# Experts' outputs of a mixture of experts: from a table in DRAM to sums on the chip, with all lists of 32 places

## The chip, the core and the metric

The kernel runs on one core of a Trainium2 chip. The metric is device time in microseconds (us) of one execution. The core has five engines that run side by side and wait for each other by semaphores: TensorE (PE; its weight loads are shown as PEld), VectorE (DVE), ScalarE (ACT), GpSimd (POOL) and SyncE (SP, which here only starts transfers). Products go to PSUM, eight banks of 512 numbers in each of 128 partitions; SBUF holds the rest.

## The reference

Two blocks one after the other on 512 tokens of 1024 numbers; only the end of the second is touched:

```
def hierarchical_moe(h, ...):                 # h: rmsnorm of x, 512 tokens
    grp = argmax(group_logits)                # one of 4 groups
    top_val, top_idx = top_k(expert_logits of that group, 2)
    gate = p_grp * softmax(top_val)
    # every token goes to 2 of 32 experts
    a = xb @ w_gate[e]; u = xb @ w_up[e]      # 1024 -> 512, twice
    y = (silu(a) * u) @ w_down[e]             # 512 -> 1024
    out[token] += y * gate
x = x + hierarchical_moe(rmsnorm(x), ...)
return rmsnorm(x, final_norm_g)
```

The inputs are drawn once, and so the routing is fixed. Counted from the reference on these inputs, 28 of 32 experts get tokens. Ten get more than 32: 179, 118, 109, 94, 70, 68, 66, 64, 48 and 38; the other 18 get 1 to 29.

## The kernel before

The mixture of experts comes last. Its three stages follow each other: routing (`route_block`, `order`), a loop over experts (`expert`), and `combine`.

**Routing** makes, by products with 0/1 matrices, a list of tokens for every expert: the first 32 places in one table, the places beyond in a second one, in blocks of 64. The experts are put in an order by their counts (`place`), so that large and small ones alternate; the largest is the seventh (e = 6), the last four have no tokens and are skipped.

**The loop.** The weights of an expert are three pieces of 2 MB: gate and up (two pieces, `wgu`) and down (`wdn`). They stand in a ring of 10 pieces (`self.ring`); `reload` has SP start piece q + 10 once piece q was used, with at most four 1 MB transfers under way. For each expert:

- `gather` (POOL starts it, four experts ahead) fetches the rows of the 32 tokens from `h2d`; each token is four rows of 256 numbers, so that 4 x 32 partitions are filled. `to_t` transposes them (PE) and scales them (DVE).
- `gate_up` makes the products with gate and up: 32 matmuls of 32 tokens by 256 columns, four side by side in the 128 columns of the array (the trace shows two instructions for each fp32 product). ACT takes the silu, DVE multiplies (`a`), `act_t` transposes (PE) and copies (DVE).
- `down` makes the products with down (16 matmuls), ACT copies them to `yo`, and POOL writes the rows to a table in DRAM, `yd`, at an address for each (token, choice) (`yi`).
- `down` of expert e runs one step late, after `gate_up` of e + 1 (`prev`), while ACT and DVE work on e + 1.
- `more` handles the places beyond 32 in blocks of 64, under `tc.If(n > b)`. An expert with few tokens jumps over this code. A block is 32 matmuls for gate and up in two halves, two transposes, 8 matmuls of 512 columns for down, and a write to `yd`.

**`combine`** reads all of `yd` (4 MB), multiplies by the gates, adds both choices to the residual `self.x` (DVE, ACT and POOL), takes the rms norm and writes the result.

The order of instructions on each engine in the loop is the order of the code (`tc.manual_schedule`).

Of the kernel before, what the change touches and what calls it, by code (L numbers as in the profile page):

```python
# [76 lines left out]
class Kern:  # L77
# [951 lines left out]
    def moe_open(self):  # L1029
# [10 lines left out]
        self.yd = self.dp.tile([8 * T, 256], F32, name="yd")  # L1040
# [7 lines left out]
        self.spacer = mp.tile([1, 1], F32, name="spacer")  # L1048
# [3 lines left out]
        self.part = mp.tile([128, 2], I32, name="part")  # L1052
        self.off = mp.tile([128, 2], F32, name="off")
        for i, n in enumerate((4, 2)):
            for g in range(n):
                r = slice(g * 128 // n, (g + 1) * 128 // n)
                nc.vector.memset(self.part[r, i:i + 1], g)
                nc.vector.memset(self.off[r, i:i + 1], float(2048 * n + g))

        self.yi, self.xi = [[mp.tile([128, 32], I32, name=f"{nm}0")] for nm in ("yi", "xi")]  # L1060
        self.hv = (self.h2d, self.h2d.rearrange("(r h) c -> r (h c)", h=2))
# [9 lines left out]
    def route_consts(self, cp):  # L1071
# [7 lines left out]
        self.iota = cp.tile([128, 2, 128], F32, name="iota")  # L1079
        for i, n in enumerate((4, 2)):  # L1080
            nc.gpsimd.iota(self.iota[:, i], pattern=[[0, n], [1, 128 // n]], base=0, channel_multiplier=0,
                           allow_small_or_imprecise_dtypes=True)
# [13 lines left out]
        self.val = cp.tile([128, NB, 2], F32, name="val")  # L1096
        nc.gpsimd.iota(self.val, pattern=[[256, NB], [1, 2]], base=-2048, channel_multiplier=2,
# [40 lines left out]
    def route_block(self, tb):  # L1138


        nc, mp, sm = self.nc, self.ro, self.sm
# [14 lines left out]
        le = mp.tile([128, 3, 32], F32, name="le", tag="le", bufs=2)  # L1156
# [10 lines left out]
        V.tensor_scalar(m[:, 4:8], self.iota[:, 0, 0:4], m[:, 0:1], NEG, op0=ALU.not_equal, op1=ALU.mult)  # L1167
        yield 1
        V.tensor_tensor(le[:, 0].rearrange("p (g e) -> p g e", g=4), lg[:, 8:40].rearrange("p (g e) -> p g e", g=4),
                        m[:, 4:8, None].to_broadcast([128, 4, 8]), op=ALU.add)  # L1170
        yield 1
        V.max(r[:, 8:16], le[:, 0])
        yield 1
        V.max_index(ix[:, 8:16], r[:, 8:16], le[:, 0])
# [3 lines left out]
        for k in range(2):  # L1178
            V.tensor_scalar(le[:, 1 + k], self.iota[:, 0, 0:32], m[:, 1 + k:2 + k], None, op0=ALU.is_equal)
        yield 1  # L1180
        V.tensor_tensor(self.OH[:, tb], le[:, 1], le[:, 2], op=ALU.add)
# [5 lines left out]
        for k in range(2):  # L1187
            V.scalar_tensor_tensor(le[:, 0], p[:, 0:32], 1.0, le[:, 1 + k], op0=ALU.mult, op1=ALU.mult,
                                   accum_out=m[:, 8 + k:9 + k])
# [3 lines left out]
        for k in range(2):  # L1193
            row = mp.tile([128, 128], F32R, name="row", tag=f"row{k}", bufs=2)
            V.tensor_scalar(row, self.iota[:, 0], m[:, 8 + k:9 + k], None, op0=ALU.is_equal)
            col = mp.tile([128, 32], F32R, name="col", tag=f"col{k}", bufs=2)
            V.tensor_scalar(col, le[:, 1 + k], self.val[:, tb, k:k + 1], None, op0=ALU.mult)
            ends = dict(stop=tb == NB - 1 and k == 1, skip_group_check=True)
            mm(self.pt[0][:, 0:4], row, col[:, 0:4], start=tb == 0 and k == 0, **ends)
            mm(self.pt[0][0:32, 128:256], col, row, start=False, **ends)  # L1200
        yield 1
        if tb == NB - 1:
            self.index(0, self.pt[0][:, 0:3], slice(0, 3))
            self.gather(self.xg0, self.xi[0][:, 0:1], 4)
# [3 lines left out]
        V.tensor_scalar(n[:, 18:20], n[:, 16:18], 63, None, op0=ALU.bitwise_and)  # L1208
        V.tensor_scalar(n[:, 20:22], n[:, 16:18], 6, None, op0=ALU.logical_shift_right)
# [3 lines left out]
        for k in range(2):  # L1213
            E = (V, P)[k]
            row = mp.tile([128, 128], F32R, name="rowb", tag=f"row{k}", bufs=2)
            V.tensor_scalar(row, self.iota[:, 1], m[:, 10 + k:11 + k], None, op0=ALU.is_equal)
            bv = mp.tile([128, 8], F32, name="bv", tag=f"bv{k}", bufs=2)
            E.tensor_scalar(bv, self.iota[:, 0, 0:8], m[:, 12 + k:13 + k], self.val[:, tb, k:k + 1], op0=ALU.is_equal,
                            op1=ALU.mult)
            col = mp.tile([128, 8, 32], F32R, name="colb", tag=f"colb{k}", bufs=2-k)  # L1220
            E.tensor_tensor(col, le[:, 1 + k, None, :].to_broadcast([128, 8, 32]),
                            bv[:, :, None].to_broadcast([128, 8, 32]), op=ALU.mult)
            for i in range(2):
                mm(self.pt[1][:, i * 128:i * 128 + 128], col[:, i * 4:i * 4 + 4, :].rearrange("p b e -> p (b e)"), row,
                   start=tb == 0 and k == 0 and i == 0, stop=tb == NB - 1 and k == 1, skip_group_check=True)

    def xindex(self, x, y, i, n):
        V = self.nc.vector
        V.tensor_scalar(x, y, 3 - i, 2 - i, op0=ALU.logical_shift_right, op1=ALU.logical_shift_left)
        V.tensor_tensor(x, x, self.part[:, i:i + 1].to_broadcast([128, n]), op=ALU.bitwise_or)  # L1230

    def index(self, i, src, c):

        y, x = self.yi[i], self.xi[i]
        self.nc.vector.tensor_scalar(y[:, c], src, (4.0, 2.0)[i], self.off[:, i:i + 1], op0=ALU.mult, op1=ALU.add)
        c = slice(c.start, min(c.stop, x.shape[1]))
        self.xindex(x[:, c], y[:, c], i, c.stop - c.start)

    def gather(self, xg, ix, G):
        self.nc.gpsimd.indirect_dma_start(out=xg, out_offset=None, in_=self.hv[G == 2],  # L1240
                                          in_offset=bass.IndirectOffsetOnAxis(ap=ix, axis=0),
                                          bounds_check=G * T - 1, oob_is_err=False)

    def gates(self, mp):
# [10 lines left out]
        V.tensor_tensor(self.gate[:, :, 1:2], self.gate[:, :, 0:1], g[:, :, 4:5], op=ALU.mult)  # L1255

# [15 lines left out]
    def moe(self):  # L1272
        nc, tc, A = self.nc, self.tc, self.A
        mm, V = nc.tensor.matmul, nc.vector
        self.shut()
        with self.pool("moe3") as m3:
            self.ring.append(m3.tile([128, 4, 1024], F32, name="ring9"))
            R, LV, LAST = 10, 3, 28
            self.yi.append(m3.tile([128, 256], I32, name="yi1"))
            self.xi.append(m3.tile([128, 32 * LV], I32, name="xi1"))  # L1280
            yi, xi, index, xindex, gather, hv = self.yi, self.xi, self.index, self.xindex, self.gather, self.hv

            def order(place, eno):
# [4 lines left out]
                T0, T1, k = xhs[2][0:32, 0:128], xhs[2][:, 128:384], xhs[2][:, 384:448]  # L1288
                nc.scalar.copy(T0, self.pt[0][0:32, 128:256])
                nc.scalar.copy(T1, self.pt[1][:, 0:256])  # L1290
# [9 lines left out]
                perm, cn = xtv[:, 0:128], xtv[0:32, 128:256]  # L1300
                V.tensor_scalar(perm, place.rearrange("p b e -> p (b e)"), own[:, 3:4], None, op0=ALU.is_equal)
                V.tensor_copy(cn, own[0:32, 0:1].to_broadcast([32, 128]))
                p = self.ps("at", "tables")
                mm(p[:, 0:32], T0, perm[0:32, 0:32], start=True, stop=True, skip_group_check=True)
                for i in range(2):
                    mm(p[:, 32 + i * 128:160 + i * 128], T1[:, i * 128:i * 128 + 128], perm, start=False, stop=True,
                       skip_group_check=True)
                for i, l in enumerate((cn, eno)):
                    mm(p[:, 288 + i * 32:320 + i * 32], l, perm[0:32, 0:32], start=False, stop=True,
                       skip_group_check=True)  # L1310
                index(0, p[:, 3:32], slice(3, 32))
                index(1, p[:, 32:288], slice(0, 256))
                return p[:, 288:352]
            yv = (self.yd, self.yd.rearrange("(r h) c -> r (h c)", h=2))
            xgs = [self.xg0] + [m3.tile([128, 256], F32, name=f"xga{i}") for i in range(1, 4)]
            xhs = [m3.tile([128, 512], F32, name=f"xgb{i}") for i in range(3)]
            xtn = m3.tile([128, 4, 2, 64], F32, name="xtn")
            xtv = xtn.rearrange("p i g t -> p (i g t)")
            ysts = []


            def to_t(xg, G, xt=None):

                n = KT // G
                xt = xt or m3.tile([128, n, G, 128 // G], F32, name="xt", tag=f"xt{G}", bufs=2)
                p = self.ps("at", "tp")
                for i in range(n):
                    nc.tensor.transpose(p[:, i * 128:i * 128 + 128], xg[:, i * 128:i * 128 + 128], self.ident)
                gv = self.gT.rearrange("p (g i) -> p i g", i=n)
                V.tensor_tensor(xt, p[:, 0:n * 128].rearrange("p (i g t) -> p i g t", i=n, g=G),  # L1330
                                gv[:, :, :, None].to_broadcast([128, n, G, 128 // G]), op=ALU.mult)
                return xt

            def gate_up(e, xt, G, p, q):

                n, W, C = KT // G, 128 // G, 1024 // G
                c = q * 256
                for kt in range(KT):
                    w = self.ring[(3 * e + kt // 4) % R]
                    for g in range(G):  # L1340
# [452 lines left out]
```

## Time and profile before

| what | value |
|---|---|
| median of 3 runs | 2059.64 us (2058.2 to 2063.69) |
| profiled execution, own time | 2060.64 us |
| its span, first to last instruction | 2058.9 us |
| PE busy | 1873.5 us (91%) |
| routing and lists made, about | 1541 to 1580 us |
| loop over experts | 1580.5 to 2024.5 us |
| after the last product | 2024.5 to 2058.9 us |

The span is what the rows below are counted in; 1.7 us of the profiled execution lie around it. A busy PE is one that has a matmul under way, which can be one that waits for weights or goes at half clock.

### The profile page before, as it was taken

Reading aid. Unit: us, or ns where it says so; the run is one execution under the profiler, and the core shown is the slowest. Engines: PE = TensorE matmul, PEld = TensorE weight load, DVE = VectorE, ACT = ScalarE, POOL = GpSimd, SP = SyncE. Lnnn points to the kernel's source line nnn. Section 1 sums busy time; section 2 is a strip of 40 time slices with the busy share of each in tenths; the row PEclk is TensorE's granted clock in tenths of the full one; section 3 lists DMA queues with packets and bytes.
Section 4 is the critical chain, followed back from the end, with each engine's and each line's share of the span. In section 5 each row is a group of like instructions: output and inputs, shape, how many; then the busy total and the mean of one; then the engine's idle time right before and its main releaser. Section 6 shows DMA issues by size and latency. Waiting matters only on the chain. (4 is left out here: it accounts for less than half of the span.)

```text
span 2058.9 us, 28841 instructions
## 1 busy us (share of the span) xinstructions
PE 1873.5 (91%) x11078; PEld 1432.5 (70%) x11082; DVE 950.0 (46%) x1700; ACT 764.0 (37%) x1197; POOL 335.7 (16%) x344
## 2 busy tenths in 40 slices
PE   8999999999999999899999998899896698878882
PEld 6777878888887888778888887677674354444441
DVE  5556375444436457565454436676655011101113
ACT  6547334333322577724333323455641000000002
POOL 0001111111002100011111001455112112222212
PEclk9999999999999999999999999899797799999996
DMA  5221233322232522133232232222075999999994
GB/s 184 86 82 48 86 111 97 101 98 97 92 103 77 167 66 99 36 113 99 96 96 98 92 103 72 77 82 82 32 290 200 399 374 391 390 374 415 410 406 173
DMA packets 71528, 334.20 MB, mean 162 GB/s; under 512 B 10794, under 2 KB 11018, under 8 KB 49328
## 3 DMA queue, kind: packets, MB, share of 16 engines
q1 hardware_dynamic: 62784, 310.06, 40.8%
q0 software_dynamic: 7984, 17.48, 2.5%
q10 hardware_dynamic: 576, 4.19, 0.5%
q8 instruction: 117, 1.92, 0.4%
q14 instruction: 67, 0.55, 0.1%
HBM read 348.44 MB, written 14.18 MB: 176 GB/s over the span
## 5 line engine op out<-in xcount | busy, mean ns | idle before, releaser
L149 PE MATMUL mm<-xTh,wh 128*128 128x512 f32 x1000 | 395.4, 396 | 7.1 <-ACT xTh L1630 6.1
L150 PE MATMUL mm<-xTl,wh 128*128 128x512 f32 x1000 | 392.0, 392 | 0.5 <-DVE xTl L1631 0.5
L151 PE MATMUL mm<-xTh,wl 128*128 128x512 f32 x1000 | 392.3, 392 | 0.0
L140 DVE TENSOR_TENSOR wl<-wraw,wh 128x1024 fp32r<-128x1024 f32 x195 | 240.4, 1234 | 324.6 <-ACT wh L139 323.4
L139 ACT CAST wh<-wraw 128x1024 fp32r<-128x1024 f32 x232 | 243.5, 1051 | 344.2 <-PE mm L150 206.5
L1341 PE MATMUL mm<-ring,xt 128*32 128x256 f32 (+1 forms) x2432 | 200.7, 423 | 70.2 <-PEq L1438 34.1
L1341 PEld LDWEIGHTS mm<-ring,xt 128*32 128x32 f32 (+1 forms) x2432 | 119.8, 128 | 147.1 <-issue 79.1
L149 PEld LDWEIGHTS mm<-xTh,wh 128*128 128x128 f32 x1000 | 188.9, 189 | 47.4 <-ACT xTh L1630 6.1
L150 PEld LDWEIGHTS mm<-xTl,wh 128*128 128x128 f32 x1000 | 188.9, 189 | 39.8 <-DVE xTl L1631 1.1
L151 PEld LDWEIGHTS mm<-xTh,wl 128*128 128x128 f32 x1000 | 188.8, 189 | 39.5 <-issue 0.4
L140 POOL TENSOR_TENSOR wl<-wraw,wh 128x1024 fp32r<-128x1024 f32 x37 | 92.6, 2508 | 563.9 <-ACT wh L139 440.9
L1345 DVE TENSOR_TENSOR a<-a,mm 128x128 f32<-128x128 f32 x56 | 16.1, 288 | 334.3 <-ACT a L1344 291.4
L1598 POOL TENSOR_TENSOR act<-u,g 128x512 f32<-128x512 f32 x44 | 57.0, 1295 | 432.5 <-ACT g L1597 432.5
L1344 ACT ACTIVATE a<-mm 128x128 f32<-128x128 f32 x56 | 15.6, 278 | 277.4 <-PE mm L1341 256.0
L1360 PE MATMUL dn<-ring,aT 128*32 128x256 f32 (+1 forms) x1120 | 105.9, 425 | 1.0 <-DVE aT L1351 0.8
L140 DVE TENSOR_TENSOR jitl<-act,jith 128x512 fp32r<-128x512 f32 x44 | 30.5, 692 | 131.7 <-ACT jith L139 131.7
L1365 POOL DMA_INDIRECT yd<-yo,yi x42 | 42.7, 1017 | 273.9 <-POOLq L1438 185.7
L149 PE MATMUL at<-wh,jith 128*128 128x512 f32 x220 | 85.8, 390 | 0.0
L151 PE MATMUL at<-wh,jitl 128*128 128x512 f32 x220 | 85.6, 389 | 0.0
L150 PE MATMUL at<-wl,jith 128*128 128x512 f32 x220 | 85.6, 389 | 0.0
L139 ACT CAST jith<-act 128x512 fp32r<-128x512 f32 x44 | 27.4, 623 | 137.2 <-PE y L150 126.0
L149 PE MATMUL mm<-wh,xTh 128*128 128x512 f32 x192 | 76.9, 402 | 0.7 <-ACT wh L139 0.7
(467 smaller groups left out, 3252.3 us busy)
## 6 DMA issues: line engine op xcount, KB each, us to landing
ring<-in_wgu_dram SPq DMA_DIRECT2D x126, 1024.0 KB
wraw<-in_w_dram SPq DMA_DIRECT2D x232, 512.0 KB
ring<-in_wdn_dram SPq DMA_DIRECT2D x62, 1024.0 KB
gb<-in_ln_dram POOLq DMA_DIRECT2D x8, 512.0 KB
yt<-yd ACTq DMA_DIRECT2D x4, 1024.0 KB
skew<-reld POOLq DMA_DIRECT2D x8, 320.0 KB
x<-in_xT_dram SPq DMA_DIRECT2D x8, 256.0 KB
x<-in_x_dram SPq DMA_DIRECT2D x4, 512.0 KB
```

Source lines behind the costliest of these rows:

```text
L139: nc.scalar.copy(h, src)
L140: (nc.gpsimd if spare else nc.vector).tensor_tensor(l, src, h.bitcast(F32), op=ALU.subtract)
L149: mm(out, lh, rh, start=first, stop=False)
L150: mm(out, lh, rl, start=False, stop=False)
L151: mm(out, ll, rh, start=False, stop=last)
L1341: mm(p[g * W:g * W + W, 0:256], xt[:, kt % n, kt // n, :], w[:, kt % 4, g * C + c:g * C + c + 256], start=kt == 0, stop=kt == KT - 1)
L1344: nc.scalar.activation(a, p[:, 0:128], AF.Silu)
L1345: V.tensor_tensor(a, a, p[:, 128:256], op=ALU.mult)
L1360: mm(p[g * W:g * W + W, 0:C], aTs[kt % n][:, (kt // n) * W:(kt // n) * W + W], w[:, kt, g * C:g * C + C], start=kt == 0, stop=kt == 3)
L1365: st = nc.gpsimd.indirect_dma_start(out=yv[G == 2], out_offset=bass.IndirectOffsetOnAxis(ap=ix, axis=0), in_=y, in_offset=None, bounds_che ...
L1598: nc.gpsimd.tensor_tensor(act[:, j, :], u, g, op=ALU.mult)
```

## The change

The outputs no longer go to DRAM. After `down`, ACT and DVE split the output (`dn`) into two fp32r parts, `yh` and `yl`, and DVE makes `oh`, a matrix with 1 where the token of a place is the token of a column. `spread(h)` multiplies `oh` with `yh` and `yl` and so puts the 32 output rows at their tokens: for half of the 512 tokens 16 matmuls with 32 rows, 128 columns of weights and 256 columns of data, the four column groups g on four row groups of the array and into four PSUM banks (`c4`). `add(h, ...)` then adds to the residual, times the gate of each token for this expert (`gp`, made once from the gates): one block of 128 tokens by DVE straight from PSUM, the next by ACT (to `tmp`) and POOL. A list's `spread` and `add` run in the following list: `spread(0)` in the middle of its gate and up, `spread(1)` ahead of its down. `down` is no longer one step late. PSUM is shared out anew for the loop (`c4` 4 banks, `tp` 2, `gu` 1, `dn` 1).

All lists have 32 places: `more` works in blocks of 32, through the same `block` as the first list, up to five blocks written out and a loop behind them. The tables grow to 16 blocks, and hold tokens (`tk`) beside addresses (`xi`); `yi`, `xindex` and the second layout go. `finish` takes the place of `combine`: the two `spread`s of the last list, its adds, the norm, the output.

```diff
+            def spread(h):
+                t = self.pm.tile([128, 4, 512], F32, name="c4", tag="c4", bufs=self.nc4)
+                for i in range(2):
+                    tb = 2 * h + i
+                    for y in (yh, yl):
+                        for g in range(4):
+                            r = slice(g * 32, g * 32 + 32)
+                            mm(t[:, g, i * 256:i * 256 + 256], oh[r, tb * 128:tb * 128 + 128], y[r], start=y is yh,
+                               stop=y is yl, skip_group_check=True)
+                return t
+            def add(h, t, e):
+                for i in range(2):
...
+                    if i == 0:
+                        V.scalar_tensor_tensor(x, s, g, x, op0=ALU.mult, op1=ALU.add)
+                    else:
+                        nc.scalar.activation(tmp.rearrange("p (g c) -> p g c", g=4), s, AF.Copy, scale=g)
+                        nc.gpsimd.tensor_tensor(self.x[:, tb], self.x[:, tb], tmp, op=ALU.add)
+            def block(e, xt, tc_, last, fill=None):
                 for kt in range(KT):
+                    if kt == 4 and last is not None:
+                        c = spread(0)
...
+                if last is not None:
+                    add(0, c, last)
+                a = m3.tile([128, 128], F32, name="a", tag="a", bufs=1)
                 nc.scalar.activation(a, p[:, 0:128], AF.Silu)
                 V.tensor_tensor(a, a, p[:, 128:256], op=ALU.mult)
+                if fill:
+                    fill()
+                p = ps("tp")
                 nc.tensor.transpose(p[:, 0:128], a, self.ident)
...
+                if e == 0 and last is None:
+                    self.gates(m3, perm[0:32, 0:32], tmp, ps)
+                if last is not None:
+                    c = spread(1)
                 w = self.ring[(3 * e + 2) % R]
...
+                if last is not None:
+                    add(1, c, last)
+                V.tensor_scalar(oh, tok, tc_, None, op0=ALU.is_equal)
+                nc.scalar.copy(yh, p[:, 0:256])
+                V.tensor_tensor(yl, p[:, 0:256], yh.bitcast(F32), op=ALU.subtract)
-                y = m3.tile([128, C], F32, name="yo", tag=f"yo{G}", bufs=G // 2)
-                nc.scalar.copy(y, p[:, 0:C])
-                nc.gpsimd.memset(self.spacer, 0.0)
-                st = nc.gpsimd.indirect_dma_start(
-                    out=yv[G == 2], out_offset=bass.IndirectOffsetOnAxis(ap=ix, axis=0), in_=y, in_offset=None,
...
-                if prev:
-                    ysts.append(down(*prev))
-                    reload(3 * e - 1 + R)
...
+                block(e, xts[e % 2], tk[0][:, e:e + 1], e - 1 if e else None, fill)
+                more(e, n, 0, ahead(e))
+                for q in range(3 * e, 3 * e + 3):
                     reload(q + R)
...
-                yt = mp.tile([128, 2, D], F32, name=f"yt{tb}")
-                nc.scalar.dma_start(yt.rearrange("p k c -> p (k c)"), yv[tb * 128:tb * 128 + 128, :])
...
+            cs = [spread(h) for h in range(2)]
+            def add(tb):
+                x = self.x[:, tb].rearrange("p (g c) -> p g c", g=4)
+                s = cs[tb // 2][:, :, tb % 2 * 256:tb % 2 * 256 + 256]
+                V.scalar_tensor_tensor(x, s, self.gl[:, tb:tb + 1], x, op0=ALU.mult, op1=ALU.add)
+                nc.scalar.activation(tmp, self.x[:, tb], AF.Square, accum_out=ms[:, tb, 0:1])
```

PE's instructions of one list near the end of the loop, in the program before (`mm` is the PSUM tile of gate and up, `dn` that of down, `tp` that of the transposes; L1438 is the jump over `more`; a number behind `aT`, `xga` or `ring` tells buffers apart):

```order
L1458 TENSOR_LOAD nb
L1341 MATMUL mm<-ring_10850,xt 32x256 x16
L1341 MATMUL mm<-ring_11283,xt 32x256 x16
L1328 MATMUL tp<-ident,xga_11459 128x128 x2
L1360 MATMUL dn<-ring_10849,aT_18154 32x256 x16
L1350 MATMUL tp<-ident,a 128x128
L1438 COMPARE_AND_BRANCH
```

The `dn` products stand ahead of the `tp` of `a`: they are those of the list before. PE's instructions of one list at the same place of the changed program, from the second half of `spread(0)` on (`gu` is gate and up, `c` with a number the tile `c4` of a `spread`):

```order
L1352 MATMUL c_24900<-yh,oh 128x256 x4
L1352 MATMUL c_24900<-yl,oh 128x256 x4
L1377 MATMUL gu<-ring_10847,xt_11488 32x256 x16
L1339 MATMUL tp<-ident,xga_10873 128x128 x2
L1387 MATMUL tp<-ident,a 128x128
L1352 MATMUL c_24947<-yh,oh 128x256 x4
L1352 MATMUL c_24947<-yl,oh 128x256 x4
L1352 MATMUL c_24947<-yh,oh 128x256 x4
L1352 MATMUL c_24947<-yl,oh 128x256 x4
L1398 MATMUL dn<-ring_10848,aT 32x256 x16
L1469 COMPARE_AND_BRANCH
```

The 32 products of the two spreads (16 each, here 8 of the first) stand between the halves of gate and up and between the transpose and down, and down is that of the same list. POOL's instructions of one list, and of its first block behind the jump, near the end of the loop of the program before (`yd<-yo` are the writes to DRAM):

```order
L1458 TENSOR_LOAD nb
L1240 DMA xga_11459<-h2d,xi_10882 128x256
L1364 MEMSET spacer 1x1
L1365 DMA yd<-yo,yi_10881 4096x256
L1438 COMPARE_AND_BRANCH
L1240 DMA xgb_11463<-h2d,xi_11457 128x512
L1364 MEMSET spacer 1x1
L1365 DMA yd<-yo,yi_11456 2048x512
```

And of the changed program:

```order
L1491 TENSOR_LOAD nb
L1233 DMA xga_11482<-h2d,xi_10871 128x256
L1366 TENSOR_TENSOR x<-x,tmp 128x1024 x2
L1469 COMPARE_AND_BRANCH
L1233 DMA xgb_11486<-h2d,xi_11476 128x256
L1366 TENSOR_TENSOR x<-x,tmp 128x1024 x2
L1469 UNCONDITIONAL_BRANCH
```

Where POOL started a write to DRAM, it now makes two sums of 128 x 1024 for every list.

## Rows read from the trace of the kernel before

**Rows 1.** Stretches: PE, PEld, DVE, ACT, POOL busy us (count), clock, DMA share, GB/s

```profile
1654.00:1699.00 45.00, 41.59 (x357) 24.28 (x357) 6.10 (x18) 3.63 (x11) 7.27 (x11) 1.00 0.89 363
...
1974.50:2013.00 38.50, 31.34 (x385) 17.32 (x386) 4.50 (x14) 3.10 (x9) 9.62 (x14) 0.98 0.99 399
```

**Rows 2.** What PE waited for, 1600 to 2010 us: total, times, longest

```profile
PE mm L1341 <- PEq L1438: 30.1, 8, 7.3
PE mm L1341 <- issue: 12.4, 7, 3.8
...
PE mm L1341 <- DMA ring<-in_wgu_dram: 2.1, 2, 1.1
```

**Rows 3.** Branches of line 1438: duration ns min/median/max, first, last

```profile
L1438 PEldq COMPARE_BRANCH  x52: 65/238/6835, 1589.6 to 2020.4; - x52
...
L1438 DVEq COMPARE_BRANCH  x52: 43/56/72, 1591.6 to 2022.1; - x52
```

**Rows 4.** Timeline of PE, e = 25: start, us, instruction [idle before <-releaser]

```profile
1995.19 3.66 PE L1341 MATMUL mm<-ring,xt 128*32 128x256 f32 x64 [1.33 <-ACTq L1438]
...
1999.15 1.93 PE L1360 MATMUL dn<-ring,aT 128*32 128x256 f32 x32
...
2002.15 3.66 PE L1341 MATMUL mm<-ring,xt 128*32 128x256 f32 x64 [0.81 <-DVEq L1438]
```

**Rows 5.** Timeline of e = 27, the last list

```profile
2018.74 0.84 PE L1341 MATMUL mm<-ring,xt 128*32 128x256 f32 x10
...
2019.64 0.28 ACT L1344 ACTIVATE a<-mm 128x128 f32<-128x128 f32 x1 [10.37 <-PE mm L1341]
...
2019.95 0.29 DVE L1345 TENSOR_TENSOR a<-a,mm 128x128 f32<-128x128 f32 x1 [10.58 <-ACT a L1344]
...
2021.75 0.33 PE L1350 MATMUL tp<-ident,a 128*128 128x128 f32 x1
...
2022.12 0.29 DVE L1351 COPY aT<-tp 128x128 f32<-128x128 f32 x1 [1.55 <-PE tp L1350]
...
2022.46 1.93 PE L1360 MATMUL dn<-ring,aT 128*32 128x256 f32 x32 [0.38 <-DVE aT L1351]
```

**Rows 6.** Timeline of PE, two blocks of 64 of e = 6

```profile
1673.85 7.13 PE L1341 MATMUL mm<-ring,xtn 128*64 128x256 f32 x64 [0.88 <-DVE xtn L1330]
...
1687.04 7.13 PE L1341 MATMUL mm<-ring,xtn 128*64 128x256 f32 x64 [0.87 <-DVE xtn L1330]
```

**Rows 7.** Timeline of PE, products one after another

```profile
1484.76 0.39 PE L149 MATMUL at<-xTh,wh 128*128 128x512 f32 x1
1484.99 0.39 PE L150 MATMUL at<-xTl,wh 128*128 128x512 f32 x1
...
1490.16 2.06 PE L877 MATMUL my<-v,S 128*128 128x129 f32 x17
```

**Rows 8.** Timeline of e = 0, where the gates are made

```profile
1589.15 1.93 PE L1360 MATMUL dn<-ring,aT 128*32 128x256 f32 x32 [0.38 <-DVE aT L1351]
...
1591.58 0.17 DVE L1255 TENSOR_TENSOR gate<-gate,gt 128x4 f32<-128x4 f32 x1
```

**Rows 9.** Timeline behind the loop

```profile
2024.51 0.37 ACT L1363 COPY yo<-dn 128x256 f32<-128x256 f32 x1 [2.20 <-PE dn L1360]
...
2035.44 1.28 DVE L1534 SCALAR_TENSOR_TENSOR x<-yt,gate,x 128x1024 f32<-128x1024 f32 x1 [13.04 <-DMA yt<-yd]
2036.87 2.34 POOL L1539 TENSOR_TENSOR x<-x,yt 128x1024 f32<-128x1024 f32 x1 [8.32 <-DVE x L1534]
...
2038.01 2.29 DVE L1534 SCALAR_TENSOR_TENSOR x<-yt,gate,x 128x1024 f32<-128x1024 f32 x1 [1.28 <-DMA yt<-yd]
...
2052.10 1.28 DVE L1527 SCALAR_TENSOR_TENSOR x<-x,ms,gf 128x1024 f32<-128x1024 f32 x1
...
2054.12 1.42 DVE L1527 SCALAR_TENSOR_TENSOR x<-x,ms,gf 128x512 f32<-128x512 f32 x2
```

**Rows 10.** Groups by line and shape, 1600 to 2028 us

```profile
L1360 PE MATMUL dn<-ring,aT 128*64 128x512 f32 x224 | 51.2, 598 | 0.0
```

More of the change, by code (lines that the diff above doesn't have):

```diff
@@ L1255, in gates @@
         V.tensor_tensor(self.gate[:, :, 1:2], self.gate[:, :, 0:1], g[:, :, 4:5], op=ALU.mult)
+        for k in range(2):
+            V.tensor_tensor(self.L2[:, :, k], self.L2[:, :, k], self.gate[:, :, k:k + 1].to_broadcast([128, NB, 32]),
+                            op=ALU.mult)
+        V.tensor_tensor(self.L2[:, :, 0], self.L2[:, :, 0], self.L2[:, :, 1], op=ALU.add)
+        p, gt = ps("gp"), tmp[0:32, 0:512]
+        for tb in range(NB):
+            nc.tensor.transpose(p[0:32, tb * 128:tb * 128 + 128], self.L2[:, tb, 0], self.ident)
+        nc.scalar.copy(gt, p[0:32, :])
+        p = ps("gp")
+        for tb in range(NB):
+            nc.tensor.matmul(p[:, tb * 32:tb * 32 + 32], gt[:, tb * 128:tb * 128 + 128], perm, start=tb == 0,
+                             stop=True, skip_group_check=True)
+        nc.scalar.copy(self.gp.rearrange("p t e -> p (t e)"), p[:, 0:128])
     def load_part(self, e, i, cond=None, at=None, eng=None, few=0):
@@ L1308, in order @@
[L1308 to L1315, printed above, removed]
@@ L1372, in block @@
-            def block(e, xt, ix):
-                a = [gate_up(e, xt, 2, self.ps("mm"), q) for q in range(2)]
-                aT = [m3.tile([128, 128], F32, name="aT", tag="aT", bufs=4) for q in range(2)]
-                for q in range(2):
-                    act_t(a[q], aT[q])
-                down(e, aT, ix, 2)
-            place = xhs[1][:, 0:128].rearrange("p (b e) -> p b e", b=4)
-            eno = xhs[0][0:32, 0:128]
+                p = self.pm.tile([128, 512], F32, name="dn", tag="dn", bufs=1)
@@ new lines, in block @@
+                for kt in range(4):
+                    for g in range(4):
+                        mm(p[g * 32:g * 32 + 32, 0:256], aT[:, kt * 32:kt * 32 + 32], w[:, kt, g * 256:g * 256 + 256],
+                           start=kt == 0, stop=kt == 3)
+                if last is not None:
[3 more added lines that the diff above has]
+                V.tensor_tensor(yl, p[:, 0:256], yh.bitcast(F32), op=ALU.subtract)
@@ L1431, in most, with more @@
                 r = 1 if e < 3 else 22 if e == 3 else e - 2 if e > 24 else (11 + i, 18 + i if i < 4 else 4 + i, 1 + i)[k]
-                return (min(T, 2 * T // r) + 31) // 64
-            def more(e, n, b, xt):
+                return (min(T, 2 * T // r) - 1) // 32
+            def more(e, n, b, ready):
                 last = most(e)
                 lv = min(LV, last)
-                with tc.If(n > b):
+                if b >= last:
+                    return
+                with tc.If(n > b + 1):
+                    g = xb[e % 3]
@@ L1456, in expert @@
-            def expert(e, xt, prev):
-                n = nc.values_load(nb[0:1, 1, e:e + 1], min_val=0, max_val=8)
-                a = gate_up(e, xt, 4, self.ps("mm"), 0)
+                            gather(g, xi[1][:, b * 32 + 32 + e:b * 32 + 33 + e])
+                        block(e, xts[2], tk[1][:, c], e)
+                        more(e, n, b + 1, False)
+                    else:
+                        with tc.For_i(b, n - 1) as c:
+                            ci, ct = m3.tile([128, 1], I32, name="ci", tag="ci", bufs=1), m3.tile([128, 1], F32, name="ct", tag="ct", bufs=1)
+                            V.tensor_copy(ci, xi[1][:, bass.ds(c * 32 + e, 1)])
+                            V.tensor_copy(ct, tk[1][:, bass.ds(c * 32 + e, 1)])
+                            gather(g, ci)
+                            to_t(g, xts[2])
+                            block(e, xts[2], ct, e)
@@ L1460, in expert, with fill @@
+            def expert(e):
+                n = nc.values_load(nb[0:1, 1, e:e + 1], min_val=0, max_val=16)
+                def fill():
+                    if e < 31:
+                        to_t(xgs[(e + 1) % 4], xts[(e + 1) % 2])
+                    if ahead(e):
+                        to_t(xb[e % 3], xts[2])
                 if e + 4 < 32:
-                    gather(xgs[e % 4], xi[0][:, e + 4:e + 5], 4)
+                    gather(xgs[e % 4], xi[0][:, e + 4:e + 5])
                 if e + 2 < 32 and ahead(e + 2):
-                    gather(xhs[(e + 2) % 3], xi[1][:, e + 2:e + 3], 2)
@@ L1473, in expert @@
-                act_t(a, aT)
-                if e == 0:
-                    self.gates(m3)
-                d = (e, [aT], yi[0][:, e:e + 1], 4)
-                now = e < 1
-                if now:
-                    ysts.append(down(*d))
-                more(e, n, 0, xt2)
-                for q in range(3 * e, 3 * e + 2 + now):
+                    gather(xb[(e + 2) % 3], xi[1][:, e + 2:e + 3])
+                block(e, xts[e % 2], tk[0][:, e:e + 1], e - 1 if e else None, fill)
+                more(e, n, 0, ahead(e))
@@ L1493, in moe, with finish @@
+            self.gl = m3.tile([128, NB], F32, name="gl")
             reload(R - 1)
             for e in range(LAST):
-                xt, prev = expert(e, xt, prev)
-            down(*prev)
-            reload(3 * LAST - 1 + R)
-            rest(LAST, xt)
-    def combine(self):
+                expert(e)
+            rest(LAST)
+            self.moe2.__exit__(None, None, None)
+            self.finish(tmp, spread)
+    def finish(self, tmp, spread):
         nc, V = self.nc, self.nc.vector
-        with self.pool("comb", "left") as mp:
-            yv = self.yd.rearrange("(t k h) c -> t (k h c)", k=2, h=4)
+        self.pmoe.__exit__(None, None, None)
+        with self.pool("comb", "left") as mp, self.tc.tile_pool(name="psc", bufs=1, space=PSUM) as self.pm:
+            self.nc4 = 2
```

261 lines of the change are left out of this document (108 added, 153 removed).

## The prediction

> **What bounds the kernel now.** I read first the busy time by stretches, to see whether weights or products set the pace of the loop. Near the end of the loop the DMA engines are busy 0.99 of the time at 399 GB/s, and 0.89 of it while the large expert is worked on [rows 1]. That looks like a loop that waits for weights. The second view, what PE waited for, says otherwise: between 1600 and 2010 us only 2.1 us went to a piece of the ring that had not landed, against 30.1 us behind the jump of line 1438 and 12.4 us in which the engine waited for nothing that the profile shows [rows 2]. The ring of ten pieces lies between the two: loads run without a gap, yet stay ahead of PE. So PE's own chain sets the end, but with little to spare, and a loop made shorter would soon wait for weights, while a loop made longer is paid in full.
>
> The chain of one list is in the timeline of PE [rows 4]. Gate and up start at 1995.19 and take 3.66 us; down of the list before starts at 1999.15, 0.30 us behind their end, since the transposes of the next list stand between, and takes 1.93; the transpose of `a` and the jump follow, with 0.81 us idle ahead of the next gate and up at 2002.15. A step is 6.96 us. The jump itself is normally 238 ns on PE, at worst 6835 ns; on DVE no one lasts over 72 ns [rows 3]. A block of 64 places takes 1687.04 - 1673.85 = 13.19 us [rows 6].
>
> **The change, part by part.**
>
> *(a) A list without further places.* Three things enter PE's chain.
>
> The spreads. Each is 16 products of 256 columns on 32 rows. No product of that shape is in the trace. The nearest rows are fp32r products of 512 columns on 128 rows, which start 0.23 us apart, so 256 columns are about .115; and 17 products of 129 columns with new weights each take 2.06 us, .12 each, so a product this short does not go below its weight load [rows 7]. If the four row groups work side by side, 16 products are four turns of .115, .46; if one after another, 16 x .12 = 1.92. A turn from one tile shape to the other may cost a little at each end: the nearest row is the .30 us between gate and up and down, which holds two transposes [rows 4], so I bound it by 0 and .15 at each of two ends. That gives .46 to 2.22. Gate and up and down themselves run four products side by side on four column groups, and 64 instructions of 256 columns take 3.66, .057 each, half of .115 [rows 4]: so this array does work side by side on tiles, and I take the lower end with half of the turns' cost, .46 + .29 (rounded up) = .75.
>
> [...]
>
> Down that is no longer late. Before, silu, product, transpose and copy lay beside down of the list before. Now they are in the chain. The last list shows them: gate and up end at 2019.58, silu starts at 2019.64 and takes .28, the product ends at 2020.24, the transpose takes .33, the copy .29, and down starts .71 behind the start of the transpose [rows 5]. The first part, 2020.24 - 2019.58, is .66, with the semaphore .70; the next list's transposes (.30) now lie in it and no longer cost anything. The copy lies beside `spread(1)`.
>
> So a list is 3.66 + .75 + .70 + .33 + .75 + 1.93 + .83 (jump) = 8.95, against 6.96: +1.99, times 27 lists **+54 us**. By the bounds of a spread: 2 x (.46 - .75) makes it 8.37, +38; 2 x (2.22 - .75) makes it 11.89, +133.
>
> The sums of DVE, ACT and POOL stand beside this. DVE from PSUM is taken as 1.28 for 128 x 1024, ACT the same; POOL takes 2.34, and DVE 2.29 when both read SBUF [rows 9]. A list asks two of each: DVE about 3 with `oh` and `yl`, POOL 4.7 and its gather, under 8.95. If that cover went, a list would be as long as POOL's work (below).
>
> *(b) Further places.* Before, 14 blocks of 64 by 13.19 are 185 us; down alone was 224 products by 598 ns in 14 x 16 instructions [rows 10]. Now 22 blocks of 32, which have no jump behind them that is taken: 8.95 - .83 = 8.1. The ten first ones are ready: 10 x 8.1 = 81. Eight are later ones of e = 6, 9 and 12: their rows come early, but the transposes and scaling stand at the start, where before .88 were idle for it [rows 6]; transposes .33 and copies on top, I take +1.35: 8 x 9.45 = 76. Four are second blocks of e = 15, 18, 21 and 24, whose gather starts only when the block does; the nearest row is the `yo` rows that come back from DRAM behind the loop, far longer than one gather, so I take about 5 us between 0 and 10: 4 x 13.1 = 52. Sum 209: **+24 us** (+4 to +44).
>
> *(c) The gates at e = 0.* Before, gates were ready at 1591.75, and down of e = 0 had started at 1589.15 without them [rows 8]. Now the products that turn gates into columns stand ahead of it on PE: 1591.75 - 1589.15 = 2.6 and as much again for the new products and copies, **+5** (0 to +7).
>
> *(d) Tables and routing.* 16 blocks where fewer stood, a few short products and copies, two layouts less: +1.5 (-2 to +4).
>
> *(e) The end.* Behind the last product there are 34.5 us now: a copy, the write and the reading of `yd`, which ends 13.04 us of idle time of DVE at 2035.44, then adds, norms and output [rows 9]. Afterwards: `yl` .9, jump 3.7 (between .24 and 6.8 [rows 3]), two spreads .9, four adds of 1.28, four scalings of 1.28 and .6 for each root, 12.6, and the output 3.4 as now (2058.9 behind 2054.12 + 1.42). Together 21.5: **-13** (-9 to -17).
>
> Sum: 54 + 24 + 5 + 1.5 - 13 = **+71.5**. Against the profiled execution's 2060.6 this is 2132; the median of the runs is 1.0 below it, so **2131**.
>
> **Rivals.**
>
> *The loop stays paced by its weights.* DMA share .99 [rows 1] speaks for it: PE's extra work might fill time in which it would otherwise have waited. Then only the ends count: 2060.6 - 13 + 1.5, and the 4 MB that are no longer written are 10 us of DMA at 399 GB/s: 2039. Against it speaks that PE waited 2.1 us for the ring [rows 2]; it decides if more than 60 us of the stalls behind line 1438 turn out to have been weights. Chance .12 (.10 faster, .02 no change).
>
> *Spreads one after another.* The row groups don't work side by side, 2.22 each: 49 lists and blocks by 2 x 1.47 are +144 on the forecast: 2275. Chance .09.
>
> *Longer jumps.* Code behind `tc.If` grows, since every block carries spreads and sums and up to five are written out. PE's stalls behind line 1438, 30.1 us in 8 waits [rows 2], become some 17 of that length: +35, 2166. The row shows only that the worst branch on PE takes 6835 ns where the median takes 238 [rows 3]. [...] Chance .10.
>
> *The sums set the pace.* POOL's 2 x 2.34, a gather, and waits for DVE on a shared path (2.29 where 1.28 is usual [rows 9]) reach 10 us a list: 49 x 1 = +49, 2180. It decides from 8.95 us of POOL a list on. Chance .07.
>
> **How the numbers follow.** The forecast has .62, with its own range of 2095 to 2185: .1 us in a spread is 98 x .1 = 9.8 us, which gives 28 down and 45 up, and the second blocks 20 either way. The range for 8 in 10 leaves out most of the serial case and half of the hidden one: 2065 to 2230. A measurement of this kernel tells .3%, 6 us, from no change. Faster: .10 from the hidden case. Same: .02 from it and .02 from the low end of the forecast. Slower: .86.
>
> **What would show it.** In the timeline of PE: a list without further places 8.95 us from gate and up to gate and up; 16 products of a spread in .75 (right under 1.0, serial near 2); idle time ahead of the transpose of `a` about .4; PE's waits for the ring still near nothing, DMA share below .9. The largest line of waits stays the jump. Behind the loop some 21 us. The prediction is wrong if gate and up wait for the ring in the changed kernel, if ACT, DVE or POOL release most of PE's waits, or if a spread is far from .75.

## The result, and the profile after

The changed kernel takes 2263.8 us (2262.1 to 2270.3), 1.0978 times the kernel before [1.0953, 1.1004]; its profiled execution has a span of 2260.4. It is slower, as forecast, but by 204 us where 71.5 were forecast, and outside the range.

The stretches of the loop, with the columns of [rows 1]:

```profile
1700.00:1800.00 100.00, 69.62 (x1151) 39.57 (x1155) 37.63 (x63) 23.47 (x36) 51.70 (x28) 0.97 0.60 238
...
1900.00:2000.00 100.00, 66.75 (x979) 36.83 (x983) 31.05 (x51) 18.62 (x28) 41.69 (x23) 0.86 0.80 316
...
2100.00:2200.00 100.00, 64.36 (x986) 35.28 (x974) 33.33 (x55) 21.27 (x32) 42.86 (x22) 0.90 0.50 193
```

The weights press less: between 1700 and 2200 us the DMA engines are busy 0.50 to 0.80 of the time (0.85 from the start of the loop, 1589.10, to 1700). But PE is busy only two thirds of it, and no other engine more than 52%. Everything waits. What PE waited for between 1600 and 2290 us (total, times, longest), against [rows 2]:

```profile
PE gu L1377 <- PEq L1469: 76.6, 16, 6.8
PE tp L1387 <- DVE a L1383: 44.0, 39, 3.6
PE tp L1339 <- DMA xgb<-h2d,xi: 27.0, 6, 6.0
PE gu L1377 <- issue: 20.2, 8, 6.5
PE gu L1377 <- DVEq L1469: 13.7, 8, 1.7
...
PE tp L1387 <- DVE xt L1341: 9.0, 10, 1.0
```

Nothing waits for the ring. The largest line is the jump (L1469 is now the one over `more`), 76.6 us in 16 waits. Second come waits ahead of the transpose of `a`, 44.0 + 9.0 us, which have no row in [rows 2]. The last list shows where those come from (timeline of three engines, to be read beside [rows 4, 5]):

```profile
2225.49 2.36 PE L1377 MATMUL gu<-ring,xt 128*32 128x256 f32 x32 [1.71 <-DVEq L1469]
...
2227.78 0.39 PE L1352 MATMUL c<-yh,oh 32*128 32x256 f32 x4
2228.01 0.29 PE L1352 MATMUL c<-yl,oh 32*128 32x256 f32 x4
2228.12 0.29 PE L1352 MATMUL c<-yh,oh 32*128 32x256 f32 x4
2228.24 0.28 PE L1352 MATMUL c<-yl,oh 32*128 32x256 f32 x4
...
2228.46 1.93 PE L1377 MATMUL gu<-ring,xt 128*32 128x256 f32 x32
2228.58 1.28 DVE L1363 SCALAR_TENSOR_TENSOR x<-c,gp,x 128x1024 f32<-128x1024 f32 x1 [3.40 <-PE c L1352]
2229.98 1.11 ACT L1365 ACTIVATE tmp<-c,gp 128x1024 f32<-128x1024 f32 x1 [5.26 <-DVE x L1363]
...
2231.00 0.27 ACT L1382 ACTIVATE a<-gu 128x128 f32<-128x128 f32 x1
2231.30 0.29 DVE L1383 TENSOR_TENSOR a<-a,gu 128x128 f32<-128x128 f32 x1 [1.43 <-ACT a L1382]
...
2231.64 0.33 PE L1387 MATMUL tp<-ident,a 128*128 128x128 f32 x1 [0.88 <-DVE a L1383]
```

The spread is as forecast: its 16 products go from 2227.78 to 2228.46, .68 us, far from the 1.92 of 16 products one after another, so the row groups do work side by side. Gate and up end at 2230.39 (2228.46 + 1.93), but silu starts at 2231.00: on ACT the copy of the spread stands ahead of it, and that copy starts only when DVE's sum has ended. The sums of the second half delay `yh` in the same way, and the next list waits 1.71 where the forecast had .83.

Behind the loop (2234.51) 25.9 us are left, against 34.5, and the first list starts at 1589.10, against 1580.49. These two cancel, so the loop alone holds the whole difference: 645.4 us for 443.9 (from the first gate and up to the end of the last down).

### The profile page after: what moved, and what is told of

It reads as the page before. It is cut to its first block, busy times and chain, and to the rows that moved or that the text cites. A ratio compares the mean times of both kernels' runs of the same rounds, so it can differ in the third digit from the quotient of the medians.

```text
span 2260.4 us, 34492 instructions
## 1 busy us (share of the span) xinstructions
PE 1951.0 (86%) x13684; PEld 1476.8 (65%) x13688; DVE 1109.3 (49%) x1887; ACT 859.9 (38%) x1295; POOL 524.9 (23%) x367
## 5 line engine op out<-in xcount | busy, mean ns | idle before, releaser
L1377 PE MATMUL gu<-ring,xt 128*32 128x256 f32 x3200 | 233.6, 435 | 125.7 <-PEq L1469 76.6
L1366 POOL TENSOR_TENSOR x<-x,tmp 128x1024 f32<-128x1024 f32 x98 | 231.5, 2362 | 278.3 <-ACT tmp L1365 278.3
L1365 ACT ACTIVATE tmp<-c,gp 128x1024 f32<-128x1024 f32 x98 | 109.2, 1114 | 487.2 <-DVE x L1363 484.3
L1377 PEld LDWEIGHTS gu<-ring,xt 128*32 128x32 f32 x3200 | 114.2, 122 | 217.9 <-issue 145.0
L1363 DVE SCALAR_TENSOR_TENSOR x<-c,gp,x 128x1024 f32<-128x1024 f32 x98 | 125.8, 1284 | 252.8 <-PE c L1352 252.8
L1398 PE MATMUL dn<-ring,aT 128*32 128x256 f32 x1600 | 99.2, 389 | 0.0
L150 PE MATMUL mm<-wl,xTh 128*128 128x512 f32 x192 | 76.2, 397 | 2.4 <-POOL wl L140 2.4
```

Source lines behind the costliest of these rows:

```text
L150: mm(out, lh, rl, start=False, stop=False)
L1363: V.scalar_tensor_tensor(x, s, g, x, op0=ALU.mult, op1=ALU.add)
L1365: nc.scalar.activation(tmp.rearrange("p (g c) -> p g c", g=4), s, AF.Copy, scale=g)
L1366: nc.gpsimd.tensor_tensor(self.x[:, tb], self.x[:, tb], tmp, op=ALU.add)
L1377: mm(p[g * 32:g * 32 + 32, 0:256], xt[:, kt % 2, kt // 2, :], w[:, kt % 4, g * 256:g * 256 + 256], start=kt == 0, stop=kt == KT - 1)
L1398: mm(p[g * 32:g * 32 + 32, 0:256], aT[:, kt * 32:kt * 32 + 32], w[:, kt, g * 256:g * 256 + 256], start=kt == 0, stop=kt == 3)
```

## The experiments

Each was run in turn with the kernel before, and a ratio is to that kernel. Its median was 2059.9 us beside the changed kernel and 2062.4 to 2064.3 beside the experiments, so a difference between two kernels that did not run side by side is good to some 4 us. The first three ask which of two things holds the missing 130 us: the sums on DVE and ACT (theory 1), or the jumps (theory 2, a rival of the prediction).

**a_split: the sums cut by columns.** Both engines get a half of each token block, so that both can read at once.

```diff
-                    if i == 0:
-                        V.scalar_tensor_tensor(x, s, g, x, op0=ALU.mult, op1=ALU.add)
-                    else:
-                        nc.scalar.activation(tmp.rearrange("p (g c) -> p g c", g=4), s, AF.Copy, scale=g)
+                    V.scalar_tensor_tensor(x[:, 0:2], s[:, 0:2], g, x[:, 0:2], op0=ALU.mult, op1=ALU.add)
+                    nc.scalar.activation(u, s[:, 2:4], AF.Copy, scale=g)
```

> The changed kernel with the sums cut by columns in place of token blocks: DVE takes the first two PSUM banks of a spread, ACT (with POOL behind it) the other two, so that both can read at once; the products and the amount of work are the same. Theory 1 (ACT's copy waits for DVE's sum because both read the same banks, and silu and yh wait behind it): the idle time ahead of the transpose of a falls from 0.9 and 1.25 us to about 0.3 and 0.65, and gate and up behind a join start about 0.6 earlier; 49 x 0.6 + up to 28 x 0.6 = 29 to 46 us less, about 2225. Theory 2 (what is missing in the forecast is all behind the jumps): within 6 us of 2264.

2328.5 us, 1.1279 [1.1247, 1.1312]: 65 us slower than the changed kernel. Both theories had it wrong. The timeline of one spread says why:

```profile
2282.13 0.75 DVE L1362 SCALAR_TENSOR_TENSOR x<-c,gp,x 128x512 f32<-128x512 f32 x1 [5.61 <-PE c L1352]
2283.00 0.69 ACT L1363 ACTIVATE tmp<-c,gp 128x512 f32<-128x512 f32 x1 [6.94 <-DVE x L1362]
...
2283.72 0.75 DVE L1362 SCALAR_TENSOR_TENSOR x<-c,gp,x 128x512 f32<-128x512 f32 x1 [0.84 <-ACT tmp L1363]
2284.50 0.69 ACT L1363 ACTIVATE tmp<-c,gp 128x512 f32<-128x512 f32 x1 [0.82 <-DVE x L1362]
```

The two engines still take turns, although they now read different halves of the tile (`c4`): ACT's copy starts at 2283.00, released by DVE's sum (2282.13 + .75), and so on. So the chain has four links in place of two, and is longer. That it makes the kernel slower by 65 us shows that this chain is on the path: the waits of the transpose for `a` rise from 44.0 to 69.6. The step is repeated below with two tiles.

**a_exact: only the code that runs.** For the routing of this input the same work; code for other routings is left out.

```diff
-                last = most(e)
+                last = {6: 5, 9: 3, 12: 3, 15: 2, 17: 1, 18: 2, 20: 1, 21: 2, 23: 1, 24: 2}.get(e, 0)
```

> The changed kernel, but the code for places beyond 32 stands only where this input runs it (ten experts, 22 blocks); the 18 other experts have no such code and no jump. For this input the same work is computed. Theory 2 (jumps over code that does not run, with the fetch of code behind them): the waits of PE behind line 1469 (76.6 us) and without a named cause (23 us) fall to under 30, and with gate and up at full pace behind them and 18 joins less the time falls by about 100 us, to 2160. Theory 1 (only the sums): the joins of 18 lists go, 18 x 1.7 = 31 us at most, about 2233.

2119.4 us, 1.0273 [1.0249, 1.0298]: 144 us less than the changed kernel, more than theory 2 expected. All waits behind the jump are gone, and gate and up run faster, in the same 3200 products (first the changed kernel, then this one; the group of line 1377):

```profile
L1377 PE MATMUL gu<-ring,xt 128*32 128x256 f32 x3200 | 233.6, 435 | 125.7 <-PEq L1469 76.6 <-issue 20.2 <-DVE xt L1341 15.1
```

```profile
L1377 PE MATMUL gu<-ring,xt 128*32 128x256 f32 x3200 | 201.6, 394 | 13.8 <-DVE xt L1341 13.8
```

The waits give 76.6 + 20.2 + 13.7 = 110.5 us (the third from the view of waits), the pace 233.6 - 201.6 = 32. The pace hangs on the waits. In the changed kernel PE is idle for 6.77 us behind a jump, and the half of gate and up that follows takes 3.64 us instead of 1.93, at a granted clock of 0.50; then the clock is 0.99 again (timeline of PE, and the stretches around it with the columns of [rows 1]):

```profile
1856.65 3.64 PE L1377 MATMUL gu<-ring,xt 128*32 128x256 f32 x32 [6.77 <-PEq L1469]
```

```profile
1856.60:1860.30 3.70, 3.65 (x36) 1.69 (x36) 0.00 (x0) 0.00 (x0) 0.03 (x1) 0.50 0.89 311
1860.30:1867.00 6.70, 5.70 (x101) 3.55 (x105) 3.97 (x7) 1.34 (x3) 2.37 (x1) 0.99 1.02 428
```

The profile also counts what the instruction queue of the DMA engines moved (its largest queue of that kind; packets, MB, share of 16 engines; first the changed kernel, then this one):

```profile
q8 instruction: 156, 2.56, 0.5%
```

```profile
q8 instruction: 110, 1.80, 0.3%
```

So 46 packets of 16 KB of instructions go with the code. In the trace of the changed kernel such packets lie where the long waits are: of the 19 starts of a list that wait over 2 us behind a join, 18 have at least one packet that starts within the wait; of the 8 that wait 1.7 us, two have one.

A list in this kernel takes 8.36 us from gate and up to gate and up (the forecast without its jump: 8.12):

```profile
1724.91 1.91 PE L1377 MATMUL gu<-ring,xt 128*32 128x256 f32 x32
...
1733.27 1.91 PE L1377 MATMUL gu<-ring,xt 128*32 128x256 f32 x32
```

**a_tiny: jumps over tiny bodies.** As a_exact, but the 18 small experts keep a jump, over one transpose and three small copies.

> As the kernel without the code that does not run, but the 18 experts keep a jump over a tiny body (one transpose, three small copies). Theory 2a (the cost is the fetch of code behind a long body): the long waits stay away, and only the joins come back, 18 x 1.7 = 31 us over the kernel without jumps, about 2190. Theory 2b (the cost is the jump itself): 2264, as before the cut.

2134.1 us, 1.0338 [1.0313, 1.0362]: 14.7 us over a_exact, .8 for each of 18 joins (1.7 were expected), and 130 us below the changed kernel. The queue of instructions moves 110 packets, as in a_exact. So jumping costs little; it is the long body that costs.

**a_pe: long bodies for PE alone.**

```diff
-                        nc.tensor.transpose(q[:, 0:128], xts[2][:, 0], self.ident)
+                        for k in range(66 * min(most(e), LV + 1)):
+                            mm(q[0:32, 0:256], xts[2][:, 0, 0, :], self.ring[0][:, 0, 0:256], start=True, stop=True)
```

> As the kernel with jumps over tiny bodies, but each of the 18 bodies that are jumped over holds for PE alone about as many instructions as the changed kernel's (66 products for each block); they are never run. If the cost is PE's own fetch of code behind a long body, most of the 130 us between the tiny bodies and the changed kernel come back: 2220 to 2264. If it is the other engines' code, 2134 as with the tiny bodies.

2205.0 us, 1.0684 [1.0652, 1.0716]: products that are never run bring back 71 of the 130 us, less than the 86 expected at the least, and with them PE's waits behind the jump. The queue of instructions moves 135 packets, 25 more than with the tiny bodies, although no engine runs an instruction more. The rest was open.

```profile
PE gu L1377 <- PEq L1468: 64.4, 13, 6.4
```

**a_ten: the ten large experts keep all their code.** The tiny bodies in place of the code of the 18 others alone.

> The changed kernel, with tiny bodies in place of the code that isn't run for the 18 small experts alone; the ten large ones keep all their blocks and the loop behind them, run or not. If the fetch of code is paid at each jump over a long stretch, wherever it is, the 59 us that PE's code for the 18 left open (2264 - 2205) lie in the ten: 2134 + 59 = 2193. If they lie in the other engines' code of the 18: 2134.

2194.7 us, 1.0639 [1.0617, 1.0661], 61 us over a_tiny, with 128 packets of instructions for 110. With the 71 of a_pe that makes 132 of 130: for the 18 the other engines' code needs no part; in the ten the engines were not told apart. The ten run their blocks and then jump over those that they don't need and the loop.

```profile
PE gu L1377 <- PEq L1477: 22.0, 6, 4.4
PE gu L1377 <- issue: 17.8, 5, 6.3
```

**b_exact: the kernel before, with the same cut.**

> The kernel before with the same cut: code for places beyond 32 only where it runs. Theory 2 (jumps cost the kernel before its 34 + 17 us of waits too): up to 50 us less, 2010, if PE sets the pace. Against it: the DMA engines are busy 0.99 of the time at 399 GB/s, and if weights then set the pace, the gain is under 20 us, 2040 to 2055, with new waits for the ring.

2039.5 us, .9885 [.9862, .9908], 24.5 us less, nearer to the 20 of the second case than to the 50 of theory 2. Its waits behind the jump are gone too, but PE now catches up with the weights, which had cost 2.1 us [rows 2]:

```profile
PE mm L1341 <- DMA ring<-in_wgu_dram: 27.5, 19, 4.4
```

**b_loop3: a shorter body in the kernel before.** The first three experts keep the loop alone.

```diff
-                lv = min(LV, last)
+                lv = min(LV if e > 2 else 0, last)
```

> The kernel before, with all further places of the first three experts in the loop alone instead of three blocks written out and the loop: shorter bodies to jump over, still right for any routing. The three waits behind them are 3.94 + 7.34 + 5.19 us: if a shorter body is fetched in less, 5 to 12 us less, 2050 to 2057; if the length doesn't matter, or the ring takes the gain, 2062.

2063.8 us, 1.0002 [.9990, 1.0014]: no change. Waits behind the jump fall from 30.1 [rows 2] to 15.6, and those for the ring rise from 2.1 to 11.7: of what is saved early, two thirds are paid to the weights, and most of the rest to waits without a name, which rise from 12.4 to 16.2.

```profile
PE mm L1341 <- PEq L1438: 15.6, 6, 3.9
PE mm L1341 <- DMA ring<-in_wgu_dram: 11.7, 7, 4.4
```

**a_split2: two PSUM tiles.** The step of a_split again, with a tile of two banks for each engine.

```diff
-                t = self.pm.tile([128, 4, 512], F32, name="c4", tag="c4", bufs=self.nc4)
+                t = [self.pm.tile([128, 2, 512], F32, name=f"c4{k}", tag=f"c4{k}", bufs=self.nc4) for k in range(2)]
```

> The changed kernel with each spread's target cut into two PSUM tiles of two banks, one read by DVE alone and one by ACT alone, so that ACT's copy no longer has to wait for DVE's sum; products and amount of work as before. Theory 1 (the chain DVE's sum, ACT's copy, then silu or yh is on PE's path): idle time ahead of the transpose of a falls from 0.9 and 1.25 us to about 0.3 and 0.7, starts behind joins come 0.6 earlier: 29 to 46 us less, 2218 to 2235. Rival (it lies beside other work): within 6 us of 2264.

2246.8 us, 1.0882 [1.0842, 1.0923], 17 us less (20 by the ratios), below the 29 that theory 1 expected at the least. ACT now starts right behind the spread, released by PE: in the last list its two copies run from 2212.33 to 2213.60, beside a sum of DVE from 2212.88 to 2213.62. The transpose of `a` waits 23.9 us in all, not 44.0. But the starts behind the joins come no earlier:

```profile
PE gu L1376 <- PEq L1468: 93.2, 21, 6.3
PE tp L1386 <- DVE a L1382: 23.9, 39, 2.4
...
PE gu L1376 <- issue: 13.1, 6, 5.8
...
PE gu L1376 <- DVEq L1468: 6.7, 5, 1.9
```

The waits ahead of gate and up behind a join are 93.2 + 13.1 + 6.7 = 113.0 us, for 110.5 before: some that ended with DVE's branch now end with PE's own. And gate and up take 7.6 us longer than in the changed kernel.

**a_early: rows of second blocks fetched early.** `many(e)` is true for all.

> The changed kernel, but the rows of a second block are fetched during the first one for every expert, not only for the first thirteen. The theory that four late fetches cost what the trace shows (27.0 us of waits for the rows, most of it in four waits near 5.9): 20 us less, 2244. Rival (PE then waits for something else there): no change.

2239.4 us, 1.0852 [1.0826, 1.0879], 24 us less, and the waits for the rows fall from 27.0 us to 5.4: they were paid in full.

**a_es: the last two together, for any routing.**

> The changed kernel for any routing, with the sums in parallel and all second blocks fetched early: 2264 - 17 - 24 = 2223 if the two add up, and clearly slower than before, since the jumps stay.

2227.7 us, 1.0805 [1.0781, 1.0830]. The two add up to 36 of 41 us.

**a_all: a_exact with both.**

> No code that isn't run, the sums in parallel on separate PSUM tiles, and all second blocks fetched early. From the kernel without the code that isn't run, 2119: 20 us for the fetches and 49 x 0.55 = 27 for the silu, about 2072: even so slower than the kernel before with the same cut (2039), by the spreads and the down that is no longer late.

2052.0 us, .9948 [.9929, .9967]: with the code that isn't run gone, the two steps are worth 67 us, not 47, and the exchange is 10 us faster than the kernel before, which holds all its code. With the same cut in both it is 12.5 us slower (against b_exact).

**b_now: the kernel before, with no down late.**

```diff
-                now = e < 1
+                now = e < LAST
```

> The kernel before, with down of every list at its own place, not one step late; everything else as before. By the rows, PE then waits .70 for silu and product, of which .30 lie beside transposes, and .38 for the copy, .78 in each of 27 lists: 21 us more, 2084, if PE's chain sets the pace all along. If loads of weights take it up where PE ran ahead of them, less, down to 2062.

2085.3 us, 1.0096 [1.0074, 1.0118], 20 us more (15 to 24), the 21 worked out. PE shows the two waits as separate rows:

```profile
2028.24 0.33 PE L1350 MATMUL tp<-ident,a 128*128 128x128 f32 x1 [0.34 <-DVE a L1345]
2028.95 1.93 PE L1360 MATMUL dn<-ring,aT 128*32 128x256 f32 x32 [0.38 <-DVEq L1438]
```

## Why the prediction was wrong

*What bounds the kernel: right.* PE's chain did, and a longer loop was paid in full; the hidden case fell. How close the weights are, "little to spare", is shown by b_exact and b_loop3.

*(a) A list: right but for one term.* The spreads cost .68 each (forecast .75), down at its own place costs what the rows say (b_now). The term "silu, product" was .70 and measures 1.25 (2230.39 to 2231.64): the cover that the forecast gave to DVE's and ACT's sums was counted as so many us of work in so many us of list, not as a chain with a place in it. DVE's 1.28 and then ACT's 1.11 stand between a spread and silu. The price, seen once the jumps are gone: a list of 8.36 where 8.12 were forecast, and 8.7 to 9.4 for most lists that also transpose the rows of a block or follow one.

*(a) The jump: the step that failed.* "The jump itself is normally 238 ns", taken as .83 us for every list as before. The rival "longer jumps" named the cause, and gave it +35 and a chance of .10. It cost 130 us in the changed kernel against tiny bodies (a_tiny), 144 with the joins (a_exact), against 24.5 in the kernel before (b_exact): 120 of the 133 us by which the forecast fell short. Sized by its own way, 17 waits of 3.76 us, the rival was right in the number (16 with that name) and short three times. The waits were longer, 4.8 us each, and those beside them grew too: [rows 2] has two more lines of waits at the jump,

```profile
PE mm L1341 <- DVEq L1438: 6.6, 8, 0.9
PE mm L1341 <- ACTq L1438: 6.4, 6, 1.3
```

so that all in all 55.5 us (with the 30.1 and 12.4) became 110.5. PE then goes at half pace (3.64 us where 1.93 is usual), 32 us in all. And where the kernel before had such waits, the loads used them to get ahead (without them PE waits 27.5 us for the ring, not 2.1), so that there they cost 24.5 us, less than half of their length, while here nothing is gained by them.

*What is left, 80 us for 71.5: luck in part.* With the jumps cut from both kernels, the exchange costs 2119.4 - 2039.5 = 80 us, within 9 of the forecast of the rest. But two errors cancel in it. Cut into parts by the starts of gate and up in these two traces, the blocks cost 70 us more (forecast 24), the lists 22 (forecast 59 with the gates), and the ends 13 less (forecast 11.5). Most of what the lists fall short is the 27.5 us that b_exact waits for weights.

*(b) Further places: mis-sized.* The late fetches were near: 20 us forecast, 24 by a_early. The blocks were not. Here are two blocks of e = 12 and the list behind them in a_exact, and the one block of e = 15 and the list behind it in b_exact:

```profile
1808.26 1.93 PE L1377 MATMUL gu<-ring,xt 128*32 128x256 f32 x32 [0.61 <-DVE xt L1341]
...
1818.72 1.93 PE L1377 MATMUL gu<-ring,xt 128*32 128x256 f32 x32 [1.50 <-DVE xt L1341]
...
1827.12 1.91 PE L1377 MATMUL gu<-ring,xt 128*32 128x256 f32 x32
```

```profile
1803.21 7.13 PE L1341 MATMUL mm<-ring,xt 128*64 128x256 f32 x64
...
1814.88 3.52 PE L1341 MATMUL mm<-ring,xt 128*32 128x256 f32 x60
```

A block of 32 with another one behind it takes 10.46 us, not 9.45, a last one 8.4, not 8.1; the 22 take 239 us in all, forecast 209. A last block of 64 takes 11.67, not the 13.19 of one with another behind it; the 14 take 169, forecast 185.

*(c) The gates: right.* Between the transpose of `a` and down of e = 0 there are 6.1 us (1597.71 to 1603.83), forecast 5.

*(d) Tables: right.* The loop starts 8.6 us later, for +1.5, but 5.5 of them are there before the first product of a table (1556.98 for 1551.50), and three other executions of kernels with the old tables start it at 1557.3 to 1557.8. From that product to the loop it is 32.1 us for 29.0, +3.1, within the range given.

*(e) The end: mis-sized.* It is -8.6 in place of -13, of which the way out of the loop takes a part: PE's jump is 5.98 us, not 3.7, and the spreads behind it go at half pace, at a granted clock of 0.50, .22 from four products to the next four (.12 in the loop).

```profile
2240.49 0.58 PE L1352 MATMUL c<-yh,oh 32*128 32x256 f32 x4 [5.98 <-PEq L1511]
2240.84 0.45 PE L1352 MATMUL c<-yl,oh 32*128 32x256 f32 x4
2241.06 0.45 PE L1352 MATMUL c<-yh,oh 32*128 32x256 f32 x4
```

*Other rivals.* Spreads one after another: no (.68). Sums that set the pace: not by their amount (POOL is busy 52% at most), but as a chain, which a_split and a_split2 priced in both directions, +65 and -17.

*Is the wait the fetch of code?* The runs point to it: products that are never run brought back waits of PE and packets in the queue of instructions together (a_pe, 25 packets and 71 us; a_ten, 18 and 61; the changed kernel, 46 and 130, all against a_tiny). The trace agrees: two such packets start within the wait of 6.25 us ahead of gate and up at 1764.02. That the branch waits for them is the author's inference; no row names what it waits for.

The length of the body shows in which jumps wait. All five lists of the changed kernel that jump over two blocks wait for PE's branch, 5.2 to 6.7 us; of nine that jump over one block seven wait 1.7 us for DVE's branch alone, and two wait 4.0 and 6.8 (e = 7 and e = 8 as examples):

```profile
1764.02 3.64 PE L1377 MATMUL gu<-ring,xt 128*32 128x256 f32 x32 [6.25 <-PEq L1469]
...
1776.62 1.93 PE L1377 MATMUL gu<-ring,xt 128*32 128x256 f32 x32 [1.71 <-DVEq L1469]
```

What stays open: why two of the nine wait (in a_pe it is five of nine), why the wait behind the first list is 1.74 us alone although its body is among the longest, and what fills a wait of 3 to 7 us, when a packet of instructions takes about 1.2 us on average (an estimate: 0.5% of 16 engines' span over 156 packets). No kernel here that takes any routing beats the kernel before; a_all and b_exact do, by knowing the routing.

## What to carry to other kernels

Count the code that a branch skips as part of a change: here the code for places that no list had, longer by the spreads and with five blocks written out for three, cost 120 us more than before, and the spreads that are run 49 x 2 x .68 = 67. Work that is hidden by its amount can still sit in front of the instruction that matters on its engine; follow the order on ACT and DVE, not their busy share. When two resources are close, a stall of one may be free, since the other uses it: compare a cut in both kernels before a stall is priced.

## What the runs showed of the hardware

PE's waits behind a jump depended on the length of code that never ran: 66 products for each block that were jumped over, in 18 places, cost 71 us, 3.9 us for each jump, while the same jumps over one transpose cost .8. The queue of instructions moved 135 packets with these products, 110 without. The half of gate and up that followed 6.77 us without a product took 3.64 us at a granted clock of 0.50, not 1.93, so that this wait cost 1.7 us more than its length. Four products on four row groups started .11 to .12 us behind the four ahead of them, as long as one product of that width on all rows would take by [rows 7] (half of the .23 between two of 512 columns, an estimate). A spread's first and last four took .23 and .22, so that all 16 took .68.
